# Split-weight buffers of a hybrid encoder step at 224 instead of 0 modulo 256 bytes

## The chip, the cores and the metric

One core of a Trainium2 chip runs the kernel. The metric is the time of one execution on the device in microseconds (us); the median of several runs is compared. "PE" is TensorE's matmul, "PEld" its weight load (which may overlap a matmul), "DVE" VectorE, "ACT" ScalarE, "POOL" GpSimd and "SP" SyncE, which here issues transfers.

## What is computed

One layer of an encoder trunk for 512 prompt frames and 64 sample frames (576 frames together), model width 2048, in float32:

```python
hn = rmsnorm(x, g_norm1)
proj = hn @ w_in                       # 2048 x 6144
q, k, v, gb, gc, hc = jnp.split(proj, ...)
q, k = rmsnorm(q, g_q), rmsnorm(k, g_k)          # per head, 8 heads x 128
o_attn = stick_breaking_blocks(q, k_all, v_all, P)
u = gc * hc
o_conv = gb * conv3(u)                 # 1024 channels
mix = concat(rmsnorm(o_attn, g_attn_out), rmsnorm(o_conv, g_conv_out))
x = x + mix @ w_out                    # 2048 x 2048
h2 = rmsnorm(x, g_norm2)
x = x + (silu(h2 @ w_gate) * (h2 @ w_up)) @ w_down   # 2048 x 5632, twice, and 5632 x 2048
```

It returns x, the new keys and values, and the state of the convolution, for both sets of frames. Nearly all arithmetic is in the products with w_in, w_out, w_gate, w_up and w_down.

## The kernel before

**How a product is made.** Frames and weights are each split into a high part in the type float32r and the rest, also float32r. A product is then three matmuls: high weights by high frames, low weights by high frames, high weights by low frames (`multiply`, `product`, `unit_run`, `conv_multiply`). Frames are the operand that streams through PE, always 288 of them at a time (one half of 576); a block of 128 x 128 weights is the stationary operand, which PE loads before each matmul. So there is one weight load for each matmul.

Most products are done as units of seven products in place of eight, on matrices cut into two by two blocks, with sums of weight blocks and of frame blocks formed beforehand (products are numbered `p_` 1 to 7). In the gate and up stage a unit is 7 products of 8 row pairs with 3 matmuls each, so 168 matmuls; there are 44 such units. The down stage has units of 3 to 7 row pairs.

**How weights come to PE.** A transfer from SP brings raw float32 weights into `raw_a`, `raw_b` or another raw tile. DVE forms sums in place. ACT copies a block of raw weights to float32r, which rounds it to the high part; DVE subtracts the high part from the raw weights, which gives the low part (helper `split`, L291 and L292, called by `prepare`; L1484 and L1487 in `conv_prepare`; `cast` and `low`, L784 and L787, in `unit_prepare`; `weight_split` and its callers for whole column chunks). The results go to four buffers in turn, two with the tag `whi` and two with `wlo`, each 2048 numbers or 8192 bytes in a partition. In a unit one buffer holds high and low blocks of one product; for a column chunk a `whi` buffer holds the high blocks and a `wlo` buffer the low ones. In the order of the program weights are prepared four products ahead of PE. The split buffers are written by ACT and DVE and read by DVE and PE; no transfer touches them.

**Where tiles lie.** Pools are laid out along each partition in the order in which they are opened. From the left side: `const`, `wpool`, `rpool`, `tmp`, `lpad`, then `acon` and the pools of the stages; from the right side `rpad` and then frames (`xpool`, later `ypool`, `mpool`). `wpool` holds `raw_a` first and then the four split buffers. By the addresses in the built program `raw_a` begins at 2816, the split buffers at 19200, 27392, 35584 and 43776, all multiples of 256. A weight block of 128 columns is 512 bytes, so each of them begins at a multiple of 256 too. `lpad` is 32 bytes of nothing, after which the pools of the stages begin at multiples of 256. Frames come in halves of 288 numbers, 1152 bytes, and so begin at 0 or 128 modulo 256. `rpool` holds row scales and accumulators (R and others, at 0), `tmp` small results (gs, ut, part and others, at 224 or 96 modulo 256).

**At the end** the blocks of the result are turned for storing: some by DVE, the last ones by PE (`store_y`, L2246 and L2249), with the block of the result as the stationary operand and the identity streamed.

The lines where the split buffers are taken:

```python
raw_tile = {"A": wpool.tile([P, 2, 2048], F32, tag="raw", name="raw_a", bufs=1)}
...
hi = wpool.tile([P, 2048], F32R, tag="whi", name=f"whi{i}")[:, : nk * ncol]
lo = wpool.tile([P, 2048], F32R, tag="wlo", name=f"wlo{i}")[:, : nk * ncol]
...
whl = wpool.tile([P, 2, NP, P], F32R, tag=("whi", "wlo")[slot_turn[0] % 2], name="whl")[:, :, :m]
```

Of the kernel before, what the change touches and what calls it, by code (L numbers as in the profile page):

```python
# [10 lines left out]
F32 = mybir.dt.float32  # L11
F32R = mybir.dt.float32r
# [4 lines left out]
P = 128  # L17
# [17 lines left out]
NP = KD // 2  # L35
# [73 lines left out]
def tile_hybrid_stream_step(  # L109
# [19 lines left out]
    wpool = ctx.enter_context(tc.tile_pool(name="wpool", bufs=2, side="left"))  # L129
# [1 line left out]
    tmp = ctx.enter_context(tc.tile_pool(name="tmp", bufs=2, side="left"))  # L131

    lpad = ctx.enter_context(tc.tile_pool(name="lpad", bufs=1, side="left"))
    lpad.tile([P, 8], F32, name="lpad_t")
    rpad = ctx.enter_context(tc.tile_pool(name="rpad", bufs=1, side="right"))
    small = rpad.tile([P, 56], F32, name="rpad_t")
    NB = T // 32
# [36 lines left out]

    ready = []
    raw_tile = {"A": wpool.tile([P, 2, 2048], F32, tag="raw", name="raw_a", bufs=1)}

    def weight_raw(i):
        src, nk, ncol = specs[i]
        raw = raw_tile["A"][:, 0 if len(EARLY) <= i < first_out else i % 2, : nk * ncol]  # L180
        return raw, raw.rearrange("p (k c) -> p k c", k=nk), src

    def weight_split(i):
        nk, ncol = specs[i][1:]
        hi = wpool.tile([P, 2048], F32R, tag="whi", name=f"whi{i}")[:, : nk * ncol]
        lo = wpool.tile([P, 2048], F32R, tag="wlo", name=f"wlo{i}")[:, : nk * ncol]
        ready.append((hi.rearrange("p (k c) -> p k c", k=nk), lo.rearrange("p (k c) -> p k c", k=nk)))
        return hi, lo

# [100 lines left out]
    def split(hi, lo, src, lo_eng=None):  # L290
        nc.scalar.copy(out=hi, in_=src)  # L291
        (lo_eng or nc.vector).tensor_tensor(out=lo, in0=src, in1=hi.bitcast(F32), op=ALU.subtract)  # L292
# [169 lines left out]
    with tc.manual_schedule(engines={mybir.EngineType.Activation, mybir.EngineType.DVE, mybir.EngineType.SP}):  # L462
        raw, raw3, src = weight_raw(0)
        raws[0] = raw
        hi, lo = weight_split(0)
# [317 lines left out]
    def cast(hi, src):  # L783
        nc.scalar.copy(out=hi, in_=src)  # L784

    def low(lo, src, hi):
        nc.vector.tensor_tensor(out=lo, in0=src, in1=hi.bitcast(F32), op=ALU.subtract)  # L787
# [314 lines left out]
    bt = {}  # L1102
    hfree, hregion, hst, hoper = [], {}, {}, {}
# [4 lines left out]
    def call_blocks(gone):  # L1108
        hfree.extend(gone)
        while hwanted and hfree:  # L1110
            n, c, s = hwanted.pop(0)
            q = hfree.pop(0)
            v = bt["g"] if q == 4 else raw_tile["A"][:, q // 2, q % 2 * 1024 : (q % 2 + 1) * 1024]
            v = v.rearrange("p (j c) -> p j c", c=P)
            c0 = UNIT_COLS[n][c][0] * AW + UNIT_COLS[n][c][1] * P
            nc.sync.dma_start(out=v, in_=w_in[:, c0 : c0 + P].rearrange("(j s p) c -> s p j c", s=2, p=P)[s])
            hregion[n, c, s] = q, v

    def unit_prepare(n, p_):
        st, tt = hst.setdefault(n, {"gone": []}), nc.vector.tensor_tensor  # L1120
        gone, own = st["gone"], bt["own"]
        first_sum = p_ in (6, 7) and 6 not in gone and 7 not in gone

        def raw(c, s):
            return hregion[n, c, s][1]

        if first_sum:
            tt(out=raw(1, 0), in0=raw(1, 0), in1=raw(0, 0), op=ALU.subtract)
            if p_ == 6:
                tt(out=own, in0=raw(1, 0), in1=raw(1, 1), op=ALU.add)  # L1130
        src = own if p_ in (3, 6) else raw(*{1: (0, 0), 2: (0, 1), 4: (1, 1), 5: (1, 0), 7: (1, 0)}[p_])
        bt["turn"] = bt.get("turn", 0) + 1
        whl = hoper[n, p_] = wpool.tile([P, 2, NP, P], F32R, tag=("whi", "wlo")[bt["turn"] % 2], name="whl")
        cast(whl[:, 0], src)
        if first_sum and p_ == 7:
            tt(out=own, in0=raw(1, 0), in1=raw(1, 1), op=ALU.add)
        yield 2
        low(whl[:, 1], src, whl[:, 0])
        gone.append(p_)
        if p_ in (6, 7) and not first_sum:  # L1140
            yield 1
            tt(out=raw(1, 0), in0=own, in1=raw(0, 0), op=ALU.add)
            tt(out=own, in0=raw(0, 1), in1=own, op=ALU.subtract)
        free = {4: [(1, 1)], 5: [(1, 0)]}.get(p_, [])
        if p_ in (2, 6, 7) and all(q in gone for q in (2, 6, 7)):
            free = [(0, 0), (0, 1)]
        call_blocks([hregion.pop((n, c, s))[0] for c, s in free])
# [280 lines left out]
    cturn = [0]  # L1428
# [26 lines left out]
    def conv_prepare(n, p_):  # L1455

        st, tt, m = cst.setdefault(n, {"left": 7, "gone": []}), nc.vector.tensor_tensor, NP if n < NCU else NH // 2
        gone, early = st["gone"], n < NCU  # L1460
        first_sum = early and p_ in (6, 7) and 6 not in gone and 7 not in gone
        if p_ == 1:
            _, st["a11"], st["a12"] = cregion[n, 0]
            st["at"] = {p: st[s] for p, s in ((1, "a11"), (2, "a12"))}
        at = st["at"]
        if first_sum or not early and p_ == 6:
            _, st["a21"], st["a22"] = cregion[n, 1]
            a11, a12, a21, a22 = (st[s] for s in ("a11", "a12", "a21", "a22"))
            own = bt["s1"] if early else bt["s1"][:, n % 2 * m : (n % 2 + 1) * m]
            at.update({3: own, 4: a22, 5: a21, 6: own, 7: a21} if early else {3: a12, 4: a22, 5: own, 6: a11, 7: a21})  # L1470
            if not early:
                tt(out=own, in0=a21, in1=a22, op=ALU.add)
            tt(out=a21, in0=a21, in1=a11, op=ALU.subtract)
            if not early:
                tt(out=a11, in0=own, in1=a11, op=ALU.subtract)
            elif p_ == 6:
                tt(out=own, in0=a21, in1=a22, op=ALU.add)
        if not early and p_ == 3:
            tt(out=at[3], in0=at[3], in1=at[6], op=ALU.subtract)
        src = at[p_]  # L1480
        cturn[0] += 1
        whl = wpool.tile([P, 2, NP, P], F32R, tag=("whi", "wlo")[cturn[0] % 2], name="whl")[:, :, :m]
        coper[n, p_] = whl
        nc.scalar.copy(out=whl[:, 0], in_=src)  # L1484
        if first_sum and p_ == 7:
            tt(out=at[6], in0=at[7], in1=at[4], op=ALU.add)
        tt(out=whl[:, 1], in0=src, in1=whl[:, 0].bitcast(F32), op=ALU.subtract)  # L1487
        gone.append(p_)
        if early and p_ in (6, 7) and not first_sum:
            tt(out=at[5], in0=at[6], in1=st["a11"], op=ALU.add)  # L1490
            tt(out=at[3], in0=st["a12"], in1=at[6], op=ALU.subtract)
        if p_ == 4 or (p_ in (2, 6, 7) and all(q in gone for q in (2, 6, 7)) if early else p_ == 3):
            c = int(p_ == 4)
            q = cregion.pop((n, c))[0]
            if n < NCU or (n, 1 - c) not in cregion:
                call_columns([q])
# [466 lines left out]
    slot_turn = [0]  # L1963
# [17 lines left out]
    def prepare(n, p_):  # L1981

        st = unit.setdefault(n, {"summed": -1})
        m = UNITS[n][3]
        if p_ == 1:
            st["a11"], st["a12"] = (region[n, 0][0][:, :, q, :] for q in range(2))
        if p_ == 7 and n == 0:
            one_sum(n)
            one_sum(n)
        if p_ == 6:  # L1990
            while st["summed"] != 6:
                one_sum(n)
        if p_ == 3:
            while st["summed"] != 3:
                one_sum(n)
        src = {1: "a11", 2: "a12", 3: "a12", 4: "a22", 5: "s1", 6: "a11", 7: "a21"}[p_]
        slot_turn[0] += 1
        whl = wpool.tile([P, 2, NP, P], F32R, tag=("whi", "wlo")[slot_turn[0] % 2], name="whl")[:, :, :m]
        split(whl[:, 0], whl[:, 1], st[src])
        operand[n, p_] = whl  # L2000
        if n >= NGU:

            if p_ == 1:
                summing.append(n)
            if summing and p_ != 2:
                k = summing[0]
                if unit[k]["summed"] != 6 or p_ == 6:
                    one_sum(k)
                if unit[k]["summed"] == 3:
                    summing.pop(0)  # L2010
        if p_ in (3, 4):
            st["gone"] = st.get("gone", 0) + 1
            if n < NGU:
                load_columns(region.pop((n, p_ - 3))[1])
            elif st["gone"] == 2:
                load_columns(region.pop((n, 0))[1])

    def one_sum(n):
        st = unit[n]
        if "sums" not in st:  # L2020
            st["sums"] = weight_sums(n)
        st["summed"] = next(st["sums"]) or 0
# [98 lines left out]
    for d, v in visits.items():  # L2121
        n = next(a for a, b in zip(v, v[1:]) if a >= NGU + 10 and b >= a + 4)
# [6 lines left out]
    turn = [0]  # L2129
# [252 lines left out]
```

## Time and profile before

| | |
|---|---|
| median of three runs | 2327.3 us (2325.7 to 2328.41) |
| the profiled execution | 2329.04 us, span of its instructions 2327.3 us |
| mean granted clock of PE | 0.999 |
| HBM | 303.53 MB read, 96.16 MB written, 172 GB/s over the span |
| DMA engines, SP's and ACT's transfers | 52.3% of 16 engines |
| DMA engines, POOL's transfers | 4.0% of 16 engines |

The profile is of one execution. Busy times of the engines say how long each had something to do; the chain of waits follows the work that ended last back to what released it; a group's row gives its count, the busy time, the mean duration of one in ns, and the idle time of its engine before it. Weight loads have rows of their own (PEld) and lie beside the matmul before them. Matmuls overlap each other, so the pace of PE is the distance between starts, not the duration in a row.

### The profile page before, as it was taken

What the parts mean: (1) busy time and instruction counts of PE and PEld (TensorE: products, weight loads), DVE (VectorE), ACT (ScalarE), POOL (GpSimd) and SP (SyncE); (2) the same over time, 40 slices, a digit from 0 to 9 for tenths busy, and PEclk for the clock granted to TensorE, in tenths of its full rate; (3) what the DMA queues carried; (4) which work ended last, traced back from release to release, by engine and by line L of the source; (5) the groups of instructions that cost most, each with busy time, mean ns of one, the idle gap of its engine ahead of it and who ended that gap; (6) DMA issues with size and microseconds to landing.
All of it is one profiled execution on the core that took longest, in us unless ns stands there. A gap on an engine that the chain in (4) does not pass through costs nothing.

```text
span 2327.3 us, 43744 instructions
## 1 busy us (share of the span) xinstructions
PE 2317.9 (100%) x17437; PEld 2310.7 (99%) x17437; DVE 1919.4 (82%) x2853; ACT 1161.8 (50%) x2016; POOL 284.8 (12%) x394
## 2 busy tenths in 40 slices
PE   9999999999999999999999999999999999999999
PEld 9999999999999999999999999999999999999999
DVE  8977887888877899888888888888888777887886
ACT  7535887444445564444444444444444444444444
POOL 2002343111111220000000000000000001431121
PEclk9999999999999999999999999999999999999999
DMA  8776564953389454444444444344354936886653
GB/s 277 212 207 169 151 156 107 335 182 117 111 271 238 150 175 145 155 145 134 155 130 149 141 138 154 122 153 151 116 160 138 358 114 219 218 238 198 194 133 103
DMA packets 584869, 402.54 MB, mean 173 GB/s; under 512 B 91870, under 2 KB 571864, under 8 KB 584664
## 3 DMA queue, kind: packets, MB, share of 16 engines
q1 hardware_dynamic: 574136, 378.56, 52.3%
q0 software_dynamic: 10160, 20.94, 4.0%
q8 instruction: 136, 2.23, 0.4%
q14 instruction: 69, 0.57, 0.1%
q10 hardware_dynamic: 368, 0.24, 0.0%
HBM read 303.53 MB, written 96.16 MB: 172 GB/s over the span
## 4 chain that ended last, share of the span: by engine, by line
PE 92%; DVE 3%; DMA 3%; SPq 1%; issue 1%; ACT 0%; ACTq 0%; DVEq 0%
PE psy L2028 36%; PE psw L2028 18%; PE psx L2028 9%; PE psy L1515 6%; PE pj L282 6%; PE pjo L282 4%; PE psw L1515 3%; PE psy L1162 3%; PE psx L1515 2%; PE psw L1162 1%; DMA raw_a<-in_w_in_dram 1%; PE psx L1162 1%; DMA form_dram<-hf 1%; PE po L1048 1%; PE z L920 1%
## 5 line engine op out<-in xcount | busy, mean ns | idle before, releaser
L2028 PE MATMUL psy<-h_s,whl 128*128 128x288 f32 x2787 | 411.3, 294 | 0.0
L2028 PEld LDWEIGHTS psy<-h_s,whl 128*128 128x128 f32 x2787 | 383.4, 188 | 0.0
L292 DVE TENSOR_TENSOR whl<-raw_a,whl 128x1024 fp32r<-128x1024 f32 (+4 forms) x296 | 318.5, 1077 | 57.5 <-ACT whl L291 56.6
L2028 PE MATMUL psw<-t,whl 128*128 128x288 f32 x2400 | 347.7, 295 | 0.0
L2028 PEld LDWEIGHTS psw<-t,whl 128*128 128x128 f32 x2400 | 327.3, 188 | 0.3 <-DVE whl L292 0.2
L291 ACT CAST whl<-raw_a 128x1024 fp32r<-128x1024 f32 (+4 forms) x296 | 268.1, 907 | 103.8 <-issue 35.4
L282 PE MATMUL pj<-x,whi 128*128 128x288 f32 x1248 | 272.7, 299 | 0.0
L292 DVE TENSOR_TENSOR whl<-raw_b,whl 128x1024 fp32r<-128x1024 f32 (+5 forms) x190 | 198.9, 1047 | 65.9 <-ACT whl L291 65.2
L291 ACT CAST whl<-raw_b 128x1024 fp32r<-128x1024 f32 (+5 forms) x190 | 165.5, 872 | 165.8 <-issue 72.6
L2038 ACT COPY part<-psy 128x288 f32<-128x288 f32 x242 | 96.4, 398 | 279.2 <-PE psy L2028 278.2
L282 PEld LDWEIGHTS pj<-x,whi 128*128 128x128 f32 x1248 | 207.5, 189 | 0.5
L282 PE MATMUL pj<-x,wlo 128*128 128x288 f32 x624 | 184.2, 295 | 0.0
L2028 PE MATMUL psy<-b22m,whl 128*128 128x288 f32 x1212 | 183.0, 294 | 0.0
L2028 PE MATMUL psy<-t2t,whl 128*128 128x288 f32 x1212 | 182.6, 294 | 0.0
L2028 PE MATMUL psx<-h_s,whl 128*128 128x288 f32 x1185 | 173.1, 294 | 0.0
L2028 PEld LDWEIGHTS psy<-t2t,whl 128*128 128x128 f32 x1212 | 168.0, 188 | 0.2 <-DVE whl L292 0.2
L2028 PEld LDWEIGHTS psy<-b22m,whl 128*128 128x128 f32 x1212 | 167.9, 188 | 0.0
L2028 PEld LDWEIGHTS psx<-h_s,whl 128*128 128x128 f32 x1185 | 162.5, 188 | 0.0
L291 ACT CAST whl<-s 128x1024 fp32r<-128x1024 f32 (+5 forms) x81 | 72.2, 892 | 100.8 <-PE psw L2028 100.7
L1807 POOL DMA_DIRECT2D hid_dram<-form x3 | 2.3, 752 | 971.6 <-DVE form L292 970.1
L282 PEld LDWEIGHTS pj<-x,wlo 128*128 128x128 f32 x624 | 117.4, 188 | 0.3
L2028 PE MATMUL psy<-t,whl 128*128 128x288 f32 x576 | 106.7, 295 | 0.0
(535 smaller groups left out, 4555.4 us busy)
## 6 DMA issues: line engine op xcount, KB each, us to landing
hid_dram<-form SPq DMA_DIRECT2D x147, 288.0 KB, 2.2
raw_a<-in_w_in_dram SPq DMA_DIRECT2D x31, 1024.0 KB, 5.5
raw_a<-in_w_gate_dram SPq DMA_DIRECT2D x22, 1024.0 KB, 5.7
raw_a<-in_w_up_dram SPq DMA_DIRECT2D x22, 1024.0 KB, 5.7
raw_b<-in_w_gate_dram SPq DMA_DIRECT2D x22, 1024.0 KB, 6.5
raw_b<-in_w_up_dram SPq DMA_DIRECT2D x22, 1024.0 KB, 6.4
h_s<-hid_dram SPq DMA_DIRECT2D x10, 2016.0 KB, 12.2
raw_a<-in_w_out_dram SPq DMA_DIRECT2D x16, 1024.0 KB, 5.5
```

The lines of the kernel that those rows point to most:

```text
L282: mm(ps, w_[:, k, csl], x_, start=(k == 0 and n == 0), stop=(k == nk - 1 and n == 2))
L291: nc.scalar.copy(out=hi, in_=src)
L292: (lo_eng or nc.vector).tensor_tensor(out=lo, in0=src, in1=hi.bitcast(F32), op=ALU.subtract)
L920: mm(zb(i), w[a_][:, kk], w[b_][:, q0:TP], start=(n == 0), stop=False, skip_group_check=True)
L1048: mm(w["po"][:, i * P : 512], w[a_][:, i, :], w[f"{b_}{i}"][:, : (512, 384, 256)[i]], stop=(i == 0 and n == 2), **kw)
L1162: mm(ps, whl[:, w_, j, :], x_, start=(start and j == 0 and q == 0), stop=(j == NP - 1 and q == 2), skip_group_check=True)
L1515: mm(ps, whl[:, w_, j, :], x_, start=(start and j == 0 and q == 0), stop=(j == m - 1 and q == 2), skip_group_check=True)
L1807: q.dma_start(out=hid_dram[fp][2 * n - 2 : 2 * n].rearrange("f p t -> p f t"), in_=t.bitcast(F32))
L2028: mm(ps, whl[:, w_, j, :], x_, start=(start and j == 0 and q == 0), stop=(j == len(xs_) - 1 and q == 2), skip_group_check=True)
L2038: nc.scalar.copy(out=t, in_=st["y"])
```

## The change

224 bytes of padding are put behind `raw_a` in `wpool`, so that the four split buffers begin at 19424, 27616, 35808 and 44000: 224 modulo 256 bytes. `lpad` grows from 32 to 64 bytes, so that the pools behind it move by 256 in all. Between the two lie `rpool` and `tmp`, whose tiles move by 224: R from 0 to 224 modulo 256, the tiles of `tmp` from 224 and 96 to 192 and 64. Everything in `const`, on the right side, and `raw_a` stays in place. The shape of the buffers is put into two helpers; what is taken from which tag is as before. The two programs have the same instructions in the same order on each engine, with the same waits; addresses alone differ.

```diff
-    lpad.tile([P, 8], F32, name="lpad_t")
+    lpad.tile([P, 16], F32, name="lpad_t")
...
     raw_tile = {"A": wpool.tile([P, 2, 2048], F32, tag="raw", name="raw_a", bufs=1)}
+    wpool.tile([P, 56], F32, tag="wpad", name="wpad_t", bufs=1)
+
+    def weight_tile(tag, name):
+        return wpool.tile([P, 2048], F32R, tag=tag, name=name)[:, :2048]
+
+    def unit_weights(turn):
+        return weight_tile(("whi", "wlo")[turn % 2], "whl").rearrange("p (f j c) -> p f j c", f=2, c=P)
...
-        hi = wpool.tile([P, 2048], F32R, tag="whi", name=f"whi{i}")[:, : nk * ncol]
-        lo = wpool.tile([P, 2048], F32R, tag="wlo", name=f"wlo{i}")[:, : nk * ncol]
+        hi = weight_tile("whi", f"whi{i}")[:, : nk * ncol]
+        lo = weight_tile("wlo", f"wlo{i}")[:, : nk * ncol]
...
-        whl = hoper[n, p_] = wpool.tile([P, 2, NP, P], F32R, tag=("whi", "wlo")[bt["turn"] % 2], name="whl")
+        whl = hoper[n, p_] = unit_weights(bt["turn"])
...
-        whl = wpool.tile([P, 2, NP, P], F32R, tag=("whi", "wlo")[cturn[0] % 2], name="whl")[:, :, :m]
+        whl = unit_weights(cturn[0])[:, :, :m]
...
-        whl = wpool.tile([P, 2, NP, P], F32R, tag=("whi", "wlo")[slot_turn[0] % 2], name="whl")[:, :, :m]
+        whl = unit_weights(slot_turn[0])[:, :, :m]
```

## The prediction

> **What bounds the kernel now.** I read the page's head first, then what TensorE waited for, then the chain that ended last, and last the stretch in which most of the time goes.
>
> ```profile
> span 2327.3 us, 43744 instructions
> ...
> PE 2317.9 (100%) x17437; PEld 2310.7 (99%) x17437; DVE 1919.4 (82%) x2853; ACT 1161.8 (50%) x2016; POOL 284.8 (12%) x394
> ```
>
> ```profile
> PE warm L472 <- DVE acA L308: 1.1, 1, 1.1
> PE psw L1515 <- ACT whl L1484: 1.0, 1, 1.0
> PE psw L1515 <- DVE whl L1487: 0.9, 1, 0.9
> PE psx L426 <- DMA xin<-in_x_prompt_dram: 0.7, 2, 0.4
> PE z L920 <- DVE kl L896: 0.5, 1, 0.5
> PE pot L2246 <- DVE acc L2058: 0.3, 1, 0.3
> PE psy L1515 <- DVE whl L1487: 0.2, 1, 0.2
> PE psy L1162 <- DVE whl L787: 0.2, 1, 0.2
> ```
>
> PE alone is busy for the whole span, and the list of its waits (engine, tile, line, total us, times, longest) adds up to 4.9 us. A busy PE can still be a slow PE, so the question is what sets its pace. Two rows of the chain (start us, us, what) answer that:
>
> ```profile
> 887.13 9.52 PE psy L2028 x72
> ...
> 1775.66 9.52 PE psy L2028 x72
> ```
>
> These are the same place in two gate/up units that lie 40 units apart: (1775.66 - 887.13) / 40 = 22.21 us a unit. A unit is 7 products of 8 row pairs with 3 matmuls each, 168 in all, so one matmul with its weight load takes 132.2 ns. Nothing else appears in between. The stretch itself (us, then busy time and count of PE, PEld, DVE, ACT, POOL, granted clock, DMA share, GB/s):
>
> ```profile
> 900.00:1790.00 890.00, 890.00 (x6733) 890.00 (x6732) 748.61 (x1025) 414.34 (x622) 0.00 (x0) 1.00 0.45 142
> ```
>
> DVE works 748.61 of 890 us, 84%, ACT 47%, the DMA engines 45%. So the time is 17,437 matmuls times their pace: 17,437 x 132.2 ns = 2305 us, 99% of the span. **Each nanosecond on the pace is 17.4 us, or 0.75%**; everything beside PE has room.
>
> **Part 1: PE reads its stationary operand at another address.** Nothing is added or removed; a weight block of 128 columns (512 bytes of a partition) begins at 224 instead of 0 modulo 256. Two things must be known: whether a load gets longer there, and whether a longer load would show. No weight of before lies at 224, so I look for other stationary operands that do. At the very end the output blocks are turned by PE, and there the block itself is the stationary operand. By the addresses in the built program, block d = 5 begins at 224 modulo 256 (the two loads at 2288.2), so does a quarter of d = 4 (the two at 2321.7), and d = 2 at 0 (the four from 2304.7). The view of that line in three windows gives line, engine, op, tile, count, then min/median/max ns:
>
> ```profile
> L2246 PEld LDWEIGHTS pot<-ident,acc x2: 141/141/141, 2288.2 to 2288.4; 128*128 128x128 f32 x2
> L2246 PEld LDWEIGHTS pot<-ident,acc x2: 140/141/142, 2321.7 to 2321.9; 128*128 128x128 f32 x2
> L2246 PEld LDWEIGHTS pot<-ident,acc x4: 141/141/143, 2304.7 to 2309.9; 128*128 128x128 f32 x4
> ```
>
> At 224 a load takes 141 ns, at 0 it takes 141 ns. The extremes are 1 to 2 ns apart, so these rows leave open about 1 ns a load on either side. They have one weakness: loads for a transpose are shorter than loads of weights, which take 188. Of that longer kind the trace has only starts at 0 (the weights) and at 128 (oner, a matrix of ones):
>
> ```profile
> L2028 PEld LDWEIGHTS psy<-h_s,whl 128*128 128x128 f32 x2787 | 383.4, 188 | 0.0
> ...
> L598 PEld LDWEIGHTS ss<-b22m,oner 128*128 128x128 f32 x2 | 0.4, 188 | 0.0
> ```
>
> No difference there either (the number before the last bar is mean ns). Would a longer load show? The attention matmuls have the same kind of load and other widths (start us, us, what):
>
> ```profile
> 270.60 0.39 PE L1006 MATMUL z<-ph,trir 128*128 128x512 f32 x1
> 270.83 0.39 PE L1007 MATMUL z<-pl,trir 128*128 128x512 f32 x1
> 271.06 0.33 PE L1008 MATMUL z<-s0h,neg1r 128*128 128x384 f32 x1
> ...
> 273.21 0.28 PE L920 MATMUL z<-qh,kh 128*128 128x256 f32 x1
> 273.33 0.28 PE L920 MATMUL z<-qh,kl 128*128 128x256 f32 x1
> 273.45 0.28 PE L920 MATMUL z<-ql,kh 128*128 128x256 f32 x1
> ```
>
> 512 columns follow each other at 0.23 us, 256 at 0.12, each with a new weight load. The pace grows with the columns, 0.43 ns a column, so the streamed operand sets it and not the load; and a load fits into 0.12 us, which leaves at least 12 ns of the 132.2 as cover. I take **0 us**. The ends: 1 ns of load in the open on every matmul would be +17 us, 1 ns less -17 us.
>
> **Part 2: ACT and DVE write the buffers at 224, and DVE reads the high half there.**
>
> ```profile
> L292 DVE TENSOR_TENSOR whl<-raw_a,whl 128x1024 fp32r<-128x1024 f32 x176 | 215.0, 1222 | 18.9 <-ACT whl L291 18.7
> L291 ACT CAST whl<-raw_a 128x1024 fp32r<-128x1024 f32 x176 | 185.2, 1053 | 50.2 <-issue 35.4 <-PE psx L2028 11.3 <-DVE raw_a L1976 2.1
> ```
>
> There are seven such casts and seven such subtractions in a unit. Whether 224 slows them is read from smaller operations that occur on both kinds of address: ut and gs lie in pool tmp at 96 or 224 modulo 256, ux and form in other pools at 0 or 128.
>
> ```profile
> L1877 DVE TENSOR_TENSOR ux<-ux,gs 128x288 f32<-128x288 f32 x44 | 20.0, 455 | 0.8
> L1877 DVE TENSOR_TENSOR ut<-ut,gs 128x288 f32<-128x288 f32 x44 | 19.9, 452 | 0.1
> ...
> L292 DVE TENSOR_TENSOR form<-ut,form 128x288 fp32r<-128x288 f32 x86 | 38.9, 452 | 5.7 <-ACT form L291 5.7
> L291 ACT CAST form<-ut 128x288 fp32r<-128x288 f32 x86 | 37.3, 434 | 69.7 <-DVE ut L1877 36.7 <-DMA hid_dram<-form 20.4 <-DVE ut L1815 9.2
> L292 DVE TENSOR_TENSOR form<-ux,form 128x288 fp32r<-128x288 f32 x64 | 28.8, 450 | 0.1
> L291 ACT CAST form<-ux 128x288 fp32r<-128x288 f32 x64 | 27.6, 431 | 35.4 <-ACT whl L291 13.1 <-DVE s L1970 10.4 <-DMA hid_dram<-form 7.9
> ```
>
> With all operands in tmp the product takes 452 ns, with ux in two places 455; subtraction and cast differ by 2 and 3 ns, under 1%. A hundredth of 1222 and 1053 ns is 12 and 11 ns, 14 times a unit 0.16 us, on engines with 3.5 us (DVE, 16% of 22.21) and more to spare in each unit. PE hides it: **0 us**. The cover ends only if each subtraction grew by 3.5 / 7 = 0.5 us, 41%.
>
> **Part 3: what moves along.** The words of the change are not quite met. Pools rpool and tmp lie between the weights and the 32 bytes that make the shift whole, so they too move by 224: R from 0 to 224, the tiles of tmp from 224 and 96 to 192 and 64. Engines do not mind, by the rows of part 2: **0 us**. Transfers touch these tiles too. The largest case that goes from an even start to 224 is the accumulator of output block d = 7, four of the 20 accumulating loads here:
>
> ```profile
> L2178 POOL DMA_DIRECT2D acc<-x_dram x20: 836/1043/1532, 1973.4 to 2078.5; - x20
> ...
> DMA to landing us min/median/max: 3.2/5.0/7.8
> ```
>
> Nobody is listed as waiting for them, so **0 us**; if all four took the longest time instead of the median and lay in the open, it would be 4 x 2.8 = 11 us, inside the ends of part 1. A page speaks against this part: the Trainium skill, "DMA: Bandwidth & Descriptors", section "How a descriptor splits into AXI transactions", says that a descriptor which does not start at a multiple of 256 bytes fetches from the multiple below and pays for the unused bytes. For 1152 bytes from 224 instead of 0, I estimate from that page 43 beats for 36. By that rule four loads of 5.0 us grow by a fifth, and the sum would be 4 us higher if it all lay in the open; no row of before tells the starts apart. The split weights themselves are no end of any transfer.
>
> **Sum.** The profiled execution took 2329.0 us, 1.7 more than its span; plus 0 + 0 + 0. The median of the three runs shown lies 1.7 us (0.07%) lower, so I predict that median, 2327.3.
>
> **Rivals.**
> - *Slower: the load no longer fits.* A block from 224 touches three stretches of 256 bytes instead of two. If the 188 ns loads, unlike the 141 ns ones, pay for that, it decides from the point where a load takes over 132.2 ns of PE; up to there nothing shows. With 0.12 us as the load's most, growth by an eighth (nine pieces for eight, supposing it reads 64 bytes at a time) gives 0.135, 2.8 ns over, +49 us, 2376; with 1 ns over it is 2345. For: no row shows a 188 ns load at 224. Against: the 141 ns rows, and 128 as good as 0.
> - *Faster: reads that now collide are spread.* Weights start at 0, streamed frames at 0 or 128 modulo 256. Of the 0.12 us for 256 columns, 256 x 0.43 = 110 ns are streaming, some 10 ns are not. If a tenth of that were collisions of the two reads, 1 ns would go: 2310. For: the rest is unexplained. Against: oner at 128 loads like a weight at 0.
> - *It is not what it says.* The tiles of part 3 would make the difference; as nobody waits for their transfers and their operations keep their length, this gives 2327 too.
>
> **Chances.** No change 0.67 (the last rival in it), slower 0.19, faster 0.14. Faster and slower mean by over 0.2%, about what a measurement of this kernel can tell from no change. The likeliest case alone is 2323 to 2332. The range takes in 1 ns a matmul on both sides, as far as 2311 and 2346; the rest of the slower rival, up to 2376, is left out.
>
> **What would show it.** After the change: the same 22.21 us between those places of the chain, 188 ns for loads of whl, 1222 and 1053 ns for L292 and L291, about 5 us of waits at PE. Step 1 is wrong if the unit's length differs by more than 0.05 us; the load's mean then tells which rival it is. Step 2 is wrong if L292 or L291 move by over 2%, and it costs only if PE's list of waits then names whl for more than 5 us. Step 3 is wrong if operations on ut, gs or R change by more than 1%, or if the list of PE's waits names a transfer that it does not name now.

## The result: 0.64% slower, by a slower pace of PE

The changed kernel takes 2342.28 us (median of 4 runs, 2341.97 to 2343.58) where the kernel before takes 2327.04 in the same comparison: a ratio of **1.0064, 95% interval 1.0051 to 1.0078**. The forecast of no change was wrong; the time lies inside the range.

The head of the page of after shows the same as before: PE is busy for the whole span, only the span is 13.5 us longer.

```profile
span 2340.8 us, 43744 instructions
...
PE 2333.0 (100%) x17437; PEld 2326.2 (99%) x17437; DVE 1920.0 (82%) x2853; ACT 1163.2 (50%) x2016; POOL 283.9 (12%) x394
```

Did a new wait appear? The two longest entries of PE's list of waits after the change (engine, tile, line, total us, times, longest) are short, and the whole list adds up to 3.4 us, less than the 4.9 of before. (Lines from the padding on are 7 higher than before, so L2028 is now L2035, L292 is L299 and L291 is L298.)

```profile
PE warm L479 <- DVE acA L315: 1.1, 1, 1.1
PE psw L1522 <- DVE whl L1494: 0.9, 1, 0.9
```

So PE does not wait, it is slower. The chain of waits of after has the same two places (start us, us, what):

```profile
888.95 9.60 PE psy L2035 x72
...
1784.95 9.60 PE psy L2035 x72
```

They are 896.00 us apart, 22.40 us a unit where it was 22.21, and 133.3 ns a matmul where it was 132.2. The 40 units between them carry 7.5 of the 13.5 us by which the span grew; 1.8 lie before the first place and 4.2 behind the second. The stretch from 900 to 1790 us (busy time and count of PE, PEld, DVE, ACT, POOL, granted clock, DMA share, GB/s) says it in another way: 6678 matmuls where 6733 were done, at the same granted clock of 1.00.

```profile
900.00:1790.00 890.00, 890.00 (x6678) 890.00 (x6677) 742.29 (x1014) 410.55 (x616) 0.00 (x0) 1.00 0.45 140
```

The groups by form (mean ns is the number before the last bar) show what has not changed: the weight load is recorded with 188 ns, the subtraction with 1221 for 1222, the cast with 1054 for 1053.

```profile
L2035 PEld LDWEIGHTS psy<-h_s,whl 128*128 128x128 f32 x2787 | 386.3, 188 | 0.0
...
L299 DVE TENSOR_TENSOR whl<-raw_a,whl 128x1024 fp32r<-128x1024 f32 x176 | 214.9, 1221 | 19.9 <-ACT whl L298 19.6
L298 ACT CAST whl<-raw_a 128x1024 fp32r<-128x1024 f32 x176 | 185.3, 1054 | 52.2 <-issue 35.9 <-PE psx L2035 12.4 <-DVE raw_a L1983 2.0
```

### The profile page after: what moved, and what is told of

Read it like the earlier page. It is cut to its first block, busy times and chain, and to the rows that moved or that the text cites. A ratio compares the mean times of both kernels' runs of the same rounds, so it can differ in the third digit from the quotient of the medians.

```text
span 2340.8 us, 43744 instructions
## 1 busy us (share of the span) xinstructions
PE 2333.0 (100%) x17437; PEld 2326.2 (99%) x17437; DVE 1920.0 (82%) x2853; ACT 1163.2 (50%) x2016; POOL 283.9 (12%) x394
## 4 chain that ended last, share of the span: by engine, by line
PE 95%; DVE 3%; DMA 1%; issue 0%; ACT 0%; SPq 0%; ACTq 0%; DVEq 0%
PE psy L2035 36%; PE psw L2035 18%; PE psx L2035 9%; PE pj L289 8%; PE psy L1522 6%; PE pjo L289 4%; PE psw L1522 3%; PE psy L1169 3%; PE psx L1522 2%; PE psw L1169 1%; PE psx L1169 1%; DMA form_dram<-hf 1%; PE z L927 1%; PE po L1055 1%; DVE x L452 0%
## 5 line engine op out<-in xcount | busy, mean ns | idle before, releaser
L2035 PE MATMUL psy<-h_s,whl 128*128 128x288 f32 x2787 | 415.0, 296 | 0.0
L2035 PEld LDWEIGHTS psy<-h_s,whl 128*128 128x128 f32 x2787 | 386.3, 188 | 0.0
L299 DVE TENSOR_TENSOR whl<-raw_a,whl 128x1024 fp32r<-128x1024 f32 (+4 forms) x296 | 319.4, 1080 | 57.5 <-ACT whl L298 56.4
L2035 PE MATMUL psw<-t,whl 128*128 128x288 f32 x2400 | 350.3, 296 | 0.0
L2035 PEld LDWEIGHTS psw<-t,whl 128*128 128x128 f32 x2400 | 330.1, 188 | 0.0
L298 ACT CAST whl<-raw_a 128x1024 fp32r<-128x1024 f32 (+4 forms) x296 | 268.3, 908 | 104.9 <-issue 35.9
L299 DVE TENSOR_TENSOR whl<-raw_b,whl 128x1024 fp32r<-128x1024 f32 (+5 forms) x190 | 197.7, 1040 | 71.2 <-ACT whl L298 70.2
L298 ACT CAST whl<-raw_b 128x1024 fp32r<-128x1024 f32 (+5 forms) x190 | 165.4, 872 | 172.7 <-issue 74.5
L2035 PE MATMUL psy<-b22m,whl 128*128 128x288 f32 x1212 | 184.5, 296 | 0.0
L2035 PE MATMUL psy<-t2t,whl 128*128 128x288 f32 x1212 | 184.5, 296 | 0.0
L2035 PE MATMUL psx<-h_s,whl 128*128 128x288 f32 x1185 | 175.0, 296 | 0.0
L2035 PEld LDWEIGHTS psy<-t2t,whl 128*128 128x128 f32 x1212 | 169.4, 188 | 0.0
L2035 PEld LDWEIGHTS psy<-b22m,whl 128*128 128x128 f32 x1212 | 169.4, 188 | 0.0
L2035 PEld LDWEIGHTS psx<-h_s,whl 128*128 128x128 f32 x1185 | 163.8, 188 | 0.0
L298 ACT CAST whl<-s 128x1024 fp32r<-128x1024 f32 (+5 forms) x81 | 72.3, 893 | 101.7 <-PE psw L2035 101.6
L2035 PE MATMUL psy<-t,whl 128*128 128x288 f32 x576 | 107.7, 297 | 0.0
```

Of the source, the lines that this page charges most:

```text
L2035: mm(ps, whl[:, w_, j, :], x_, start=(start and j == 0 and q == 0), stop=(j == len(xs_) - 1 and q == 2), skip_group_check=True)
```

## The experiments

Three theories stood at the start. **A**: a weight block that starts at 224 is slow to read, whatever streams past it. **B**: what counts is how the starts of weights and frames stand to each other, since PE reads both at once. **C**: it is not the reading at all, but the writes of ACT and DVE or the tiles that moved along.

### Which of the edits it is

`weights_alone` moves the split weights to 224 and leaves rpool and tmp where they were; `neighbours_alone` moves those two and leaves the weights.

```diff
 weights_alone
+    wpool.tile([P, 56], F32, tag="wpad", name="wpad_t", bufs=1)
...
+    rpool.tile([P, 8], F32, tag="gap", name="gap_t", bufs=1)
 neighbours_alone
+    rpool.tile([P, 56], F32, tag="gap", name="gap_t", bufs=1)
...
-    lpad.tile([P, 8], F32, name="lpad_t")
+    lpad.tile([P, 16], F32, name="lpad_t")
```

In `neighbours_alone` the gap stands ahead of R and the tiles of tmp.

> The split weights begin at 224, and rpool and tmp stay where they were before the change. If the weights' start is the cause (A or B): a gate/up unit of 22.40 us, and 2342 us in all (ratio 1.0064). If the tiles that moved along are the cause: a unit of 22.21 us and 2327 us.

> The split weights stay at 0, and rpool and tmp move by 224 as in the changed kernel. If the weights' start is the cause: a unit of 22.21 us and 2327 us. If the tiles that moved along are the cause: 22.40 us and 2342 us.

| | us (median, lowest to highest) | ratio to before, 95% interval |
|---|---|---|
| weights_alone | 2342.32 (2341.06 to 2344.37) | 1.0065 [1.0048, 1.0082] |
| neighbours_alone | 2325.79 (2324.8 to 2328.35) | 0.9993 [0.9984, 1.0003] |

Between the same two places of the chain a unit takes 22.40 us in `weights_alone` and 22.21 in `neighbours_alone`. The weights carry the whole loss; the tiles that move along cost nothing that shows.

### PE alone

A program with matmuls of the kernel's shape and order, and no other work beside them, separates A and B from C: nothing writes while PE runs.

```diff
+        for r in range(again):
+            for j in range(8):
+                for q, (f, h) in enumerate(((0, 0), (1, 0), (0, 1))):
+                    a = wo // 4 + (0 if one_w else 1024 * f + 128 * j)
+                    b = xo // 4 + (0 if one_x else 576 * j + 288 * h)
+                    mm(ps, w[:, a : a + P], x[:, b : b + n], start=(r + j + q == 0),
...
```

> This kernel leaves the whole layer out: PE alone works, in rows of 48 matmuls in the order of the kernel's units (high weights by high frames, low by high, high by low), with the start of the weights (w) and of the frames (x) chosen in bytes modulo 256, and with other widths of the frames (n). Theory A, the start of the weights alone sets the pace, whatever else the core does: 48 matmuls take 6.35 us between starts at w0 (132.2 ns each) and 6.40 us at w224 (133.3 ns each), with any start of the frames. Theory B, reads of weights and of frames collide, so that their distance matters: w224 with x224 is as fast as w0 with x0, and w0 with x32 or x224 is slow. Theory C, the loss comes from writes of ACT and DVE into the buffers or from the tiles that moved along: with those engines idle all rows take the same time. If the load is only hidden by cover, widths of 128 and 192 show it uncovered: there w224 is slower than w0 by more than 1 ns a matmul under A, and equal under C.

The timeline of PE (start us, us, what), rows of 48 matmuls; w224x0 means weights at 224 and frames at 0 (high half) and 128 (low half), n128 means 128 frames streamed in place of 288. The time of a row is the distance to the start of the next.

```profile
29.44 6.51 PE L39 MATMUL w0x0e<-x,w 128*128 128x288 f32 x48
35.78 6.55 PE L39 MATMUL w4x0e<-x,w 128*128 128x288 f32 x48
...
55.04 6.56 PE L39 MATMUL w32x0e<-x,w 128*128 128x288 f32 x48
61.44 6.55 PE L39 MATMUL w48x0e<-x,w 128*128 128x288 f32 x48
...
99.65 6.56 PE L39 MATMUL w224x0e<-x,w 128*128 128x288 f32 x48
106.05 6.53 PE L39 MATMUL w240x0e<-x,w 128*128 128x288 f32 x48
...
137.91 6.51 PE L39 MATMUL w0x224e<-x,w 128*128 128x288 f32 x48
144.26 6.51 PE L39 MATMUL w32x32e<-x,w 128*128 128x288 f32 x48
...
214.33 6.51 PE L39 MATMUL w224x224e<-x,w 128*128 128x288 f32 x48
220.68 5.47 PE L39 MATMUL w0n128e<-x,w 128*128 128x128 f32 x48
225.99 5.55 PE L39 MATMUL w0n192e<-x,w 128*128 128x192 f32 x48
...
276.41 5.47 PE L39 MATMUL w224n128e<-x,w 128*128 128x128 f32 x48
281.71 5.55 PE L39 MATMUL w224n192e<-x,w 128*128 128x192 f32 x48
```

Weights at 0 take 6.34 us (35.78 - 29.44; 132.1 ns a matmul), at 224 they take 6.40 (133.3): PE alone has the loss of the kernel, so C falls. Weights at 224 with frames at 224 as well take 6.35 (220.68 - 214.33), as fast as 0 with 0: that speaks for B against A. One row goes against what was expected of B: weights at 0 with frames at 224 were to be slow, and take 6.35 us (144.26 - 137.91). Weights at 32 with frames at 0 have the same two distances between the starts (224 for the high half and 96 for the low one) and take 6.40 (61.44 - 55.04). So how the starts stand to each other counts, but their distance alone does not fix the pace. And the load itself is no longer at 224: with 128 frames, where streaming is too short to hide it (192 frames take hardly longer, 112.3 ns), 48 matmuls with their loads take 5.31 us at 0 and 5.30 at 224, 110.5 ns each.

### In the kernel: other starts, and the frames moved too

`all_moved` gives the frames the same shift as the weights: the left pools of the stages by leaving `lpad` as it was, the right ones by 32 bytes more in `rpad`. The other kernels of this kind put the weights at 128, 96 and 32 with a pad and a gap that together make 256 bytes.

```diff
 all_moved
+    wpool.tile([P, 56], F32, tag="wpad", name="wpad_t", bufs=1)
-    small = rpad.tile([P, 56], F32, name="rpad_t")
+    small = rpad.tile([P, 64], F32, name="rpad_t")
 weights_at_96 (for 128: 32 and 32; for 32: 8 and 56)
+    wpool.tile([P, 24], F32, tag="wpad", name="wpad_t", bufs=1)
+    rpool.tile([P, 40], F32, tag="gap", name="gap_t", bufs=1)
```

> The split weights begin at 128, rpool and tmp stay. A block of 512 bytes then touches three stretches of 256 bytes, as from 224, but eight stretches of 64 bytes, as from 0. If stretches of 256 bytes (or of 512) decide: a unit of 22.40 us and 2342 us. If stretches of 64 or of 128 bytes decide: 22.21 us and 2327 us.

> Split weights at 224 as in the change, and all frames that stream past them moved by 224 too (the pools of the stages on the left by leaving lpad at 32 bytes, those on the right by 32 more bytes in rpad): every pair of weights and frames has the old distance modulo 256 again. Theory B (what counts is how the two starts stand to each other): the loss of 15 us goes, 2327, a unit of 22.2 us; weights alone on PE at 224 with frames at 224 took 6.35 us for 48 matmuls, as 0 with 0 did (6.34). Theory A (a weight start of 224 is slow whatever streams): 2342, a unit of 22.4 us.

> Split weights at 96, all other tiles where they were before. Theory B with the table of PE alone (96 against frames at 0 and 128: 6.32 us for 48 matmuls, 0 against them 6.34): no loss, 2327 or up to 0.4 ns a matmul less, 2320. Theory A in the form that only starts at multiples of 128 bytes are free: 2342, ratio 1.006.

> Split weights at 32, all other tiles where they were before. Theory B with the table of PE alone (32 against frames at 0 and 128: 6.40 us for 48 matmuls, as 224 took): as slow as 224, 2342, a unit of 22.4 us. A rival that only the end of a block beyond a multiple of 256 by 224 bytes costs: 2327.

| weights, frames (modulo 256) | us (median, lowest to highest) | ratio to before, 95% interval | unit, us |
|---|---|---|---|
| 224, moved by 224 (all_moved) | 2330.71 (2329.03 to 2334.16) | 1.0013 [1.0004, 1.0021] | 22.21 |
| 96, as before | 2321.28 (2320.03 to 2323.34) | 0.9970 [0.9958, 0.9981] | 22.15 |
| 128, as before | 2323.02 (2313.08 to 2326.12) | 0.9974 [0.9962, 0.9987] | 22.21 |
| 32, as before | 2343.26 (2340.4 to 2344.83) | 1.0060 [1.0044, 1.0075] | 22.40 |

The units come from the chains, as above. For `all_moved`:

```profile
884.57 9.52 PE psy L2029 x72
...
1773.10 9.52 PE psy L2029 x72
```

(1773.10 - 884.57) / 40 = 22.21. With weights at 224 the pace of before is back as soon as the frames stand at 224 too; A falls in the kernel as well. 32 is as slow as 224, so a particular end of the block is not it either. Nor is it the number of stretches that a block touches: one from 96 touches three of 256 bytes and nine of 64, as many as one from 224, and 96 is faster than 0. (One from 128 touches three of 256 too, and is no slower.) The chain at 96:

```profile
885.14 9.49 PE psy L2030 x72
...
1771.18 9.49 PE psy L2030 x72
```

(1771.18 - 885.14) / 40 = 22.15 us, 131.9 ns. **`weights_at_96` beats both kernels.** At 128 the profiled run had the unit of before, while the ten runs spread over 13 us, where those of before in the same comparison spread over 5 (2325.86 to 2331.02); more on this below. The 0.1% by which `all_moved` stays above before is not explained: the unit and the span (2327.3 us) of its profiled run are those of before, but that run was the shortest of its eleven.

### Is the distance the whole rule?

> PE alone, none of the layer's results computed: rows of 192 and 96 matmuls of 288 columns with weights at 0, 64, 112 and 224, and frames, all at one distance from them, at each of 16 distances modulo 256. Theory B in its strict form (the distance alone counts): the four rows of one distance agree within 0.3 ns a matmul, while distances differ by 1 to 3 ns. If rows of one distance disagree by 1 ns or more, the distance modulo 256 is not the whole rule, and each pair of starts has a pace of its own. Theory A: all rows at 224 are slower than all rows at 0.

Rows of 96 matmuls, in which all frames stand at one distance d from the weights modulo 256. Four distances, at weights of 0 and of 224 (timeline of PE):

```profile
296.36 13.09 PE L39 MATMUL w0d112e<-x,w 128*128 128x288 f32 x96
309.29 12.96 PE L39 MATMUL w0d128e<-x,w 128*128 128x288 f32 x96
322.08 12.65 PE L39 MATMUL w0d144e<-x,w 128*128 128x288 f32 x96
334.57 12.96 PE L39 MATMUL w0d160e<-x,w 128*128 128x288 f32 x96
...
905.99 13.09 PE L39 MATMUL w224d112e<-x,w 128*128 128x288 f32 x96
918.92 12.96 PE L39 MATMUL w224d128e<-x,w 128*128 128x288 f32 x96
931.72 12.65 PE L39 MATMUL w224d144e<-x,w 128*128 128x288 f32 x96
944.21 12.96 PE L39 MATMUL w224d160e<-x,w 128*128 128x288 f32 x96
```

At 0 and at 224 alike, distance 112 takes 12.93 us (134.7 ns a matmul), 128 takes 12.79 and 12.80 (133.3), 144 takes 12.49 (130.1). The rows with weights at 0, 64 and 224 agree within 0.02 us at all 16 distances. Those at 112 do not: 144 takes 12.69 us there, and its fastest distance is 96. So in rows with a single distance the distance decides, for the three starts that are multiples of 32 bytes; 112 is not one, being 16 more than 96.

In the order of the kernel (high frames at 0, low ones at 128), rows of 192 took 132.2 ns with weights at 0 and 133.3 at 224, each twice: exactly the paces of the two kernels. There two matmuls of three have one distance and the third has 128 more, and the table above does not foretell what they take. Its mean fits for weights at 0 (132.2) and 224 (133.4); for 96 it would be 133.4, where the row took 132.0, and for 128 it would be 132.7, where the row took 131.1. So the distance is not the whole rule.

### Next load or own weights, and how a row begins

> PE alone, none of the layer's results computed. (1) Weights at every multiple of 16 against frames in the kernel's order (high at 0, low at 128), 192 matmuls each: 0, 224, 96, 128 and 16 again at 132.2, 133.3, 132.0, 131.1 and 135.5 ns a matmul if the pace belongs to the starts; it tells whether a start better than 96 and 128 exists. (2) Rows of weights at 128 behind 1 to 7 other matmuls: 131.1 in all if the pace is fixed by the starts; some at 131.1 and others at 132.2 if it also hangs on how the row begins, which would account for the spread of the kernel with weights at 128. (3) Two weight starts by turns with two frame starts by turns, so that a matmul's own weights and the next matmul's weights stand at different distances from its frames. By the table of distances (80: 131.1, 112: 134.6, 144: 130.1, 176: 131.4): if the next weights' load collides with the running frames, next144 130.1, next112 134.6, own144 133.0 (mean of 112 and 176), own112 130.6 (mean of 80 and 144); if a matmul's own weights count, the names exchange: own144 130.1, own112 134.6, next144 133.0, next112 130.6. A load of 188 ns spans one and a half matmuls, so values between are possible and would mean both.

First the search for a better start (rows of 192 in the kernel's order, timeline of PE):

```profile
182.63 25.49 PE L39 MATMUL k96e<-x,w 128*128 128x288 f32 x192
207.96 25.13 PE L39 MATMUL k112e<-x,w 128*128 128x288 f32 x192
232.93 25.34 PE L39 MATMUL k128e<-x,w 128*128 128x288 f32 x192
258.11 26.14 PE L39 MATMUL k144e<-x,w 128*128 128x288 f32 x192
284.08 25.76 PE L39 MATMUL k160e<-x,w 128*128 128x288 f32 x192
```

112 takes 24.97 us, 130.05 ns a matmul, the best of all sixteen; 96 takes 131.9, 128 takes 131.15, 144 as much as 135.3. Second, 96 matmuls with weights at 128 behind one to seven others:

```profile
450.30 12.90 PE L39 MATMUL after2e<-x,w 128*128 128x288 f32 x96
463.04 0.45 PE L57 MATMUL filler<-x,w 128*128 128x128 f32 x3
463.32 12.80 PE L39 MATMUL after3e<-x,w 128*128 128x288 f32 x96
475.96 0.56 PE L57 MATMUL filler<-x,w 128*128 128x128 f32 x4
```

They took 131.7 ns behind three and four (475.96 - 463.32), 132.6 to 132.8 behind the others (463.04 - 450.30 behind two). From the eleventh matmul of each row on, the pace is 131.1 behind three and four and 132.2 behind the others: with the same starts there are two paces, and how the row begins decides which. On 16,800 matmuls 1 ns is 17 us, enough for the 13 us of spread in `weights_at_128`. The profiled run of that kernel has both paces: 612 matmuls start between 760 and 840 us and 607 between 1000 and 1080, where before has 607 in each. Third, the pairs answered neither expectation: own144 130.3, next144 134.3, own112 and next112 133.2 both. A matmul's own distance fits the first and not the others; the next load's distance fits none. This stays open.

### The best start in the kernel

```diff
+    weight_space = wpool.tile([P, 4 * 2048 + 32], F32R, tag="weights", name="weight_space", bufs=1)
+    weight_turn = {"whi": 0, "wlo": 2}
 def weight_tile(tag, name):
+        k = weight_turn[tag]
+        weight_turn[tag] = k ^ 1
+        return weight_space[:, 28 + 2048 * k : 28 + 2048 * (k + 1)]
```

> Split weights at 112 modulo 256, all other tiles where they were before. Since a pool begins its tiles at multiples of 32 bytes, the four buffers are parts of one tile here, taken in the same turns, from 112 bytes behind its start. Theory B with the pace of PE alone (112 against frames at 0 and 128: 130.05 ns, 0 against them 132.24): 2.2 ns less on some 17,000 matmuls, 37 us, so 2290, a unit of 21.85 us. Rival: DVE, busy 84% of the stretch before, or the transfers cannot follow, and new waits of PE take part of it back: between 2290 and 2327, with PE's waits far above the 4.9 us of before. Theory A in any form: 2327 or more.

> The same one tile for the four buffers, with their starts at 0 as before: 2327, ratio 1.000, a unit of 22.21 us, if taking the buffers from one tile costs or gains nothing. Whatever it differs by is no part of what 112 does.

In both kernels ACT and DVE take up some work in another order. By the order of the built programs 12 of the 16,800 matmuls with split weights, in a unit of w_in, find another weight block in their buffer than before, so y is not that of the layer, and these kernels serve for their times alone. The number, the shape and the order of PE's matmuls are the same. Times: 2312.16 us (2303.73 to 2316.74) at 112, ratio 0.9924 [0.9905, 0.9943]; 2337.09 (2335.35 to 2339.11) at 0, ratio 1.0037 [1.0024, 1.0050]. So the one tile costs 9 us by itself, and 112 gains 25 us against it, not the 37 expected. The 9 us are no matter of the starts: the control has two waits that before has not (engine, tile, line, total us, times, longest), and around them the granted clock falls to 0.97 between 700 and 750 us and to 0.93 between 850 and 900. In these two stretches it does 82 matmuls fewer than before, some 11 us.

```profile
PE psx L1525 <- DVE weight_space L202: 3.8, 1, 3.8
PE ss L608 <- ACT b22m L301: 2.0, 1, 2.0
```

The kernel at 112 has the same two waits. Its chain, in the units of w_in (L1526) and of gate and up (L2039):

```profile
512.22 9.36 PE psy L1526 x72
534.06 9.36 PE psy L1526 x72
...
889.73 9.44 PE psy L2039 x72
...
1770.79 9.44 PE psy L2039 x72
```

(1770.79 - 889.73) / 40 = 22.03 us, 131.1 ns. The control has 22.21, as expected. Against the control new waits explain little: PE's waits add up to 14.9 us in one and 10.0 in the other. What misses in gate and up is the pace, 131.1 for the 130.05 of PE alone. The units of w_in reach it in the same run: 534.06 - 512.22 = 21.84 us, where before has 22.21 in both stages; so do the 617 matmuls between 1880 and 1960 us, where before has 607. The starts are the same in all of them, modulo 256. So here too one pair of starts has two paces, 1.1 ns apart, and holds one of them through a stage. That the beginning of a stage chooses it, as that of a row did at 128, was not tried; the spread of the times, 13 us, is that of `weights_at_128`.

### Does it come from the load's reads?

> PE alone, none of the layer's results computed: 288 frames stream as before, but the weight block has 128, 96, 64 or 32 columns, so that the load reads that much less; weights at 0, 16, 112 and 224 against frames at 0 and 128, 192 matmuls a row. At 128 columns the paces are 132.2, 135.5, 130.05 and 133.3 ns, 5.4 between the extremes. If the load's reads get in the way of the frames' reads (collision), the spread shrinks with the columns: some 2.7 ns at 64, 1.4 at 32, and all rows come towards 130 ns or below. If the spread belongs to something that every load does whatever it reads (its start, the change-over of weights), it stays near 5.4 ns with 32 columns.

| columns of the weight block | weights at 0 | 16 | 112 | 224 | spread |
|---|---|---|---|---|---|
| 128 | 132.2 | 135.4 | 130.0 | 133.3 | 5.4 ns |
| 96 | 132.2 | 132.2 | 132.2 | 131.1 | 1.1 |
| 64 | 131.2 | 131.2 | 132.2 | 132.2 | 1.1 |
| 32 | 130.4 | 131.2 | 131.1 | 132.6 | 2.2 |

(ns a matmul from the distances of starts; the rows of 128 and 32 columns were run twice and repeat within 0.3 ns.) Fewer columns change both the size and the order of the differences: at 96 columns 224 is the fastest start, at 128 it is slower than 0. That fits reads of the load that take part in it, but does not show it by itself: with fewer columns the matmul also gives fewer rows of the result, and the record of the load is shorter (161 ns at 96 for 188 at 128). Nor does the spread shrink in proportion, and it is wider at 32 columns than at 64: the simple picture, so many colliding reads at so much each, does not hold.

**What is settled:** the loss comes from where the split weights start relative to the frames that stream past them; PE alone has it, and the loads are no longer than before. **What is open:** what in PE's two reads makes the difference, by which rule a pair of starts costs more or less, and why one pair can have two paces.

## Why the prediction was wrong

- **What bounds the kernel** was right: each nanosecond of pace is some 17 us. Measured were 1.1 ns (22.40 for 22.21 us a unit) and 15.2 us between the medians. On 16,800 matmuls, 1.1 ns makes 18.5 us; most of what lacks lies ahead of the first place of the chain, which was reached only 1.8 us later than before (the stretch of the column chunks, from 150 to 517 us, took 365.9 us for 367.0). That the time lies inside the range is luck in its cause: the range allowed 1 ns a matmul for a load in the open, and no load came into the open.
- **Part 1 is the step that failed.** It said that the pace grows with the columns, "so the streamed operand sets it and not the load", and that a load which fits has at least 12 ns of cover; "I take 0 us". Both premises hold by the runs: a load with little streaming takes 110.5 ns at 0 and at 224, some 22 ns below the pace, and its record stays at 188. The conclusion does not follow. That a load fits under a matmul says that it does not end late; it does not say that the pace is free of where the two operands lie. Measured was 133.3 ns for 132.2 with the starts alone changed. Starts exist with 130.0 ns, so some 2 of the 132.2 hang on the starts already. The Trainium skill, "TensorE: Matmul & The Clock Gate", section "Step-by-step: what each phase is for", says that loading the next weights takes no read bandwidth from the running matmul. No run here measured that bandwidth; but in the rows of distances, where nothing but the starts changed, a matmul took 130.1 to 134.7 ns, so it may not be read as saying that the starts do not matter.
- **The evidence for it measured the wrong thing.** The 141 ns loads at 224 and the 188 ns load of oner at 128 are durations of loads. They were read rightly, and the load of a weight is recorded with 188 ns in the slow kernel too. What changes is the time between the starts of matmuls, and the profile of before showed that for weights at 0 alone.
- **The rival "the load no longer fits"** had the right sign, and its milder price (2345) came near 2342, but not for its reason: no load went over 132.2 ns of PE, and by 96 the stretches that a block touches do not count. **The rival "reads that now collide are spread"** came nearest in kind, since it let the starts of the two operands matter together, but with the wrong sign: 224 is worse than 0, though 96 is better, by 0.3%. That reads collide is not shown. Its "against" (oner at 128 loads like a weight at 0) was again a load's duration.
- **Part 2 was right:** 1221 and 1054 ns for 1222 and 1053; the subtraction of form from ut stays at 452.
- **Part 3 was right:** `neighbours_alone` is at 0.9993 [0.9984, 1.0003]. The 20 accumulating loads were issued in 1040 ns for 1043 and landed in 4.9 us for 5.0 at the median. The Trainium skill's rule on descriptors, as the prediction cites it, would have made 4 us in the open. The interval ends at +0.03%, 0.7 us, so nothing of that size shows, and since nobody waits for these loads the rule itself is not decided.
- **What would show it.** The unit's length did (0.19 us off, where 0.05 was the limit), and rightly threw out part 1. That "the load's mean then tells which rival it is" was wrong: it is 188 ns in both kernels, and only PE alone, with narrow and wide matmuls, told them apart.

## What to carry to other kernels

Where PE is the bound and every matmul has its own weight load, the starts of the two operands in SBUF, one against the other, are worth up to 4% of the pace (130.0 to 135.4 ns on PE alone here) without a single wait in the profile. Read it from the distance of starts in the chain, not from the durations of loads; try it on PE alone, with the kernel's own order and shapes, which here gave the paces at 0 and 224 to 0.1 ns, and then in the kernel, since not every gain of PE alone arrives there. "It is hidden beside something else" needs a second question: does the pace of the one depend on where the other's data lie?

## What the runs showed of the hardware that was not expected

- In rows with a single distance between the two starts modulo 256, the pace goes by that distance for weights at 0, 64 and 224: 130.1 ns at 144, 134.7 at 112. For weights at 112 the table is another, and rows that mix two distances do not take the mean.
- One pair of starts can have two paces: 131.1 and 132.2 ns for weights at 128, by how many matmuls went before the row; 130.0 and 131.1 for weights at 112, by the stage of the kernel.
- The width counts too. From the rows of PE alone with weights at 0 and at 224: 384 frames took 8.43 and 8.34 us for 48 matmuls, so there 224 is the faster; 512 frames took 11.20 in both, 128 frames 5.31 and 5.30.
- The paces in the table of narrow loads come mostly in steps of about 1.1 ns: 130.0, 131.1, 132.2, 133.3. No run says what makes the step.
- A load of 128 columns with 128 frames to stream takes 110.5 ns, while its record says 192: the record of a load holds more than the time for which it keeps PE.
